# Holding four groups of mixer products later in TensorE's order, and moving elementwise work between VectorE, ScalarE and GpSimd

## The chip, the cores and the metric

The kernel runs on one core of one Trainium2 chip. A run's time is the device time of that core, in microseconds (us). TensorE (PE in the rows) does the matrix products and the transposes, VectorE is DVE, ScalarE is ACT, GpSimd is POOL, and SyncE (SP) issues nearly all DMAs.

## What is computed

Two layers over a sequence of 512 tokens of width 2048. Each layer normalises x, projects it with one large matrix, feeds four mixers of width 512, and merges them with a second large matrix:

```
h = rmsnorm(x, pre_g); proj = h @ w_in
o_a = gla_mixer(...)       # gated linear attention, chunks of 64
o_b = rglru_mixer(...)     # LRU: conv of 4 taps, gates, linear scan
o_c = nsa_mixer(...)       # sparse attention: compressed, selected, window
o_d = conformer_mixer(...) # conv of 31 taps, layernorm, silu, @ pw_w
mixed = group_rmsnorm(concat(o_a, o_b, o_c, o_d), branch_g) * silu(z gates)
x = x + rmsnorm(mixed @ w_out, post_g)
```

The LRU in full, since the change touches it (softplus(-lambda) is a vector per channel):

```
r  = sigmoid(xh @ w_a + b_a);  ig = sigmoid(xh @ w_x + b_x)
log_a = -8 * r * softplus(-lam);  a = exp(log_a)
u = sqrt(-expm1(2 * log_a)) * (ig * xc);  h = scan(h * a + u)
```

## The kernel before

Everything is kept transposed: 128 channels on the partitions, the 512 tokens along the row. A float32 product is done as three products of rounded parts (`mm3`: high*high, high*low, low*high), so each weight tile is split after it is loaded: ScalarE writes the high part `whi` (L145), VectorE or GpSimd subtracts it from the raw weights to give the low part `wlo` (L146). Which of the two engines does so is set by `pool_share`: a counter runs from 0 to 5, and a split goes to GpSimd when its number is in the tuple. `PS_A` is all six numbers, `PS_B` is (0, 3), a third.

TensorE's stream per layer: the first four columns (`f`), then 36 columns of the projection, each a sum over 16 blocks k of 128 channels, three products per block, so 48 products of 512 tokens (`pfm`, made in `proj`). In order they are 0 to 3 CONF_V, 4 to 7 LRU_X, then the products `tm` (284 wide, 16 loads of which each split is 128x284), 8 to 11 the keys and values of the sparse attention, 12 and 13 its first queries, 14 to 17 GLA's q and k, then `gv`, 18 and 19 the other queries, 20 to 35 the four gate (z) groups CONF, LRU, NSA, GLA. Then `out_ps`, the 16 columns of w_out. Between these big products stand the small ones of the mixers, which are written as Python generators (`tasks`) and advanced by a budget after each column. The chain of mixers is CONF convolutions, LRU, conformer tail, compress, group norms, attention (two rounds), its group norm, GLA, its group norm.

The order on each engine is set before the run by a planner that plays a timeline with modelled durations: big products and their accumulations have the priority "last", weight loads and splits and the evictions of columns "first", mixer work lies between. On an engine the order is then fixed, and an instruction whose inputs are late holds up all behind it. PSUM is used as eight banks: four accumulators (`acc`), three that all mixer products take in turn (`mx`), one more (`op`).

Places that the change and the prediction name: in the LRU the two gate products go to `lru_ps`, ScalarE writes sigmoid to `r` and `ig` in SBUF (L327), GpSimd multiplies `xc` by `ig` (L334) and squares `r` into `ig` (L337), VectorE makes `th` (L132, named `lth<-li,lth`), ScalarE takes its root (L340), GpSimd multiplies `xc` by it (L343), VectorE scans (L344). In the conformer tail squares are summed and split (`shi`, `slo`), the product with ones gives `var_ps`, its inverse root `lnr` (L209, L210) scales the channels (L397), Silu (L398), split, and the products `pw_ps`. In GLA `klt_ps` are four transposes, ScalarE copies them to `gklt` (L629), and `ds_ps` are seven steps of products that a chain of VectorE operations takes up (`gsp`). At the end of a layer the gated mixer outputs are split into `H` and `L` (L237, L238), which overwrite the projection's inputs, and `out_ps` reads them block by block.

Of the kernel before, what the change touches and what calls it, by code (L numbers as in the profile page):

```python
# [13 lines left out]
AF = mybir.ActivationFunctionType  # L14
# [7 lines left out]
P = 128  # L22
KT = D // P
# [35 lines left out]
PS_A, PS_B = (0, 1, 2, 3, 4, 5), (0, 3)  # L59


class Trunk:
    def __init__(self, ctx, tc, a):
        self.tc, self.nc, self.a = tc, tc.nc, a
        nc = self.nc
        self.act = nc.scalar.activation
        self.dve, self.gp = nc.vector, nc.gpsimd
        self.tr = nc.tensor.transpose
        self.bands = {"first": -2000000, "last": 2000000}
        self.tasks = []  # L70
        self.flip = 0
        self.pp = False
        self.pool_share = (0, 3)

        def pool(name, bufs, **kw):
            return ctx.enter_context(tc.tile_pool(name=name, bufs=bufs, **kw))

        con = pool("con", 1)
        self.lay = pool("lay", 1)
        self.hp = pool("hp", 1)  # L80
        self.wp = pool("wp", 3)
        self.sm = pool("sm", 4)
        self.big = pool("big", 1)
        self.acc = pool("acc", 4, space=PSUM)
        self.mx = pool("mx", 3, space=PSUM)
        self.op = pool("op", 1, space=PSUM)

        consts = con.tile([P, NCON], F32, name="consts")
        self.ident = consts[:, C_ID:C_ID + 128]
        self.tri = consts[:, C_TRI:C_TRI + 256]  # L90
        self.cmpm = consts[:, C_CMP:C_CMP + 124].rearrange("p (b n) -> p b n", b=4)
        self.glam = consts[:, C_GLA:C_GLA + 128].bitcast(U32)
        self.fold = consts[:62, C_FOLD:C_FOLD + 31]
        self.avg_d = con.tile([P, 2], F32, name="avg_d")
        self.dve.memset(self.avg_d, 1.0 / D)
        self.ones = con.tile([P, P], F32R, name="ones")
        self.dve.memset(self.ones.bitcast(F32), 1.0)
        self.consts = consts
        self.eps = con.tile([P, 1], F32, name="eps")
        self.dve.memset(self.eps, EPS)  # L100
        self.one = con.tile([P, 1], F32, name="one")
        self.dve.memset(self.one, 1.0)
        self.zero = con.tile([P, 1], F32, name="zero")
        self.dve.memset(self.zero, 0.0)
        self.warm = con.tile([P, 1], F32, name="warm")
        self.act(self.warm, self.one, AF.Exp)
        self.x1 = nc.dram_tensor("x1_scratch", (4, P, 4, S), F32, kind="Internal").ap()
# [90 lines left out]
        return self.split(self.strip("pt", "shi", 512, F32R), self.strip("pt", "slo", 512, F32R), src, self.dve)  # L198

    def mm(self, out, lhsT, rhs, start=True, stop=True, **kw):  # L200
        self.nc.tensor.matmul(out, lhsT, rhs, start=start, stop=stop, **kw)  # L201

    def mm3(self, out, ahi, alo, bhi, blo, start, stop, **kw):
        self.mm(out, ahi, bhi, start, False, **kw)
        self.mm(out, ahi, blo, False, False, **kw)
        self.mm(out, alo, bhi, False, stop, **kw)

    def rsqrt(self, out, ms, scale):
        self.act(out, ms, AF.Sqrt, bias=self.eps, scale=scale)  # L209
# [43 lines left out]
    def proj(self, c, ps=None):  # L253
        ps = self.bank("pfm", self.acc, "acc") if ps is None else ps
        u = FM_UNIT[c]
        for h in range(2):
            parts = self.unit(self.a["w_in"][self.l, u + h])
            with self.band("last"):
                for k in range(8):
                    kk = 8 * h + k  # L260
                    hi, lo = parts[k // 4]
                    w = slice(k % 4 * P, (k % 4 + 1) * P)
                    self.mm3(ps, hi[:, w], lo[:, w], self.H[kk], self.L[kk], kk == 0, kk == KT - 1)
        return ps

    def scaled(self, out, ps):
# [44 lines left out]
    def lru(self, xin):  # L311
        dve, act, gp = self.dve, self.act, self.gp
        cpos = self.lru_consts()
        xc, r, ig, th = self.quad("t2", "lxc"), self.quad("t3", "lr"), self.quad("t1", "li"), self.quad("t5", "lth")
        self.Y[LRU] = ig
        h = [slice(c * 512, (c + 1) * 512) for c in range(4)]
        yield 1.0
        for c in range(4):
            yield from self.taps(xc[:, h[c]], xin[c], 4, V_LCW + 4 * c, V_LCB + c, self.bank("lc_ps", self.op, "op"))
        whi, wlo = self.mixer_unit(self.a["lru_w"][self.l])  # L320
        for c in range(4):
            xhi, xlo = self.strip_split(xc[:, h[c]])
            for i, (o, b) in enumerate(((r, V_BA), (ig, V_BX))):
                ps = self.bank("lru_ps")
                w = slice(i * 512 + c * P, i * 512 + (c + 1) * P)
                self.mm3(ps, whi[:, w], wlo[:, w], xhi, xlo, True, True)
                act(o[:, h[c]], ps, AF.Sigmoid, bias=self.col(b + c))  # L327
            yield 1.5
        for c in range(4):
            act(th[:, h[c]], r[:, h[c]], AF.Tanh, scale=cpos[:, c:c + 1])  # L330
        self.ts(dve, cpos, cpos, -1.0, None, ALU.mult)
        for c in range(4):
            act(r[:, h[c]], r[:, h[c]], AF.Exp, scale=cpos[:, c:c + 1])
            gp.tensor_mul(xc[:, h[c]], xc[:, h[c]], ig[:, h[c]])  # L334
        yield 3.0
        for c in range(4):
            gp.tensor_mul(ig[:, h[c]], r[:, h[c]], r[:, h[c]])  # L337
        for c in range(4):
            self.stt(th[:, h[c]], ig[:, h[c]], 1.0, th[:, h[c]], ALU.add, ALU.mult)
        act(th, th, AF.Sqrt)  # L340
        yield 4.0
        for c in range(4):
            gp.tensor_mul(xc[:, h[c]], xc[:, h[c]], th[:, h[c]])  # L343
            dve.tensor_tensor_scan(ig[:, h[c]], r[:, h[c]], xc[:, h[c]], 0.0, op0=ALU.mult, op1=ALU.add)  # L344
            yield 1.5
# [23 lines left out]
    def conformer_tail(self):  # L369
        dve, gp, act, Y = self.dve, self.gp, self.act, self.Y[CONF]  # L370
        cv = [Y[:, c * 512:(c + 1) * 512] for c in range(4)]
        t_, u_ = self.strip("pt", "lnt"), self.strip("pt", "lnu")
        gp.tensor_add(t_, cv[0], cv[1])
        dve.tensor_add(u_, cv[2], cv[3])
        dve.tensor_add(t_, t_, u_)
        ps = self.chan_sum(t_, "mu_ps")
        yield 3.0
        for c in range(4):
            self.stt(cv[c], ps, -1.0 / 512, cv[c], ALU.mult, ALU.add)
            yield 0.6  # L380
        t_ = self.strip("pt", "lnt")
        act(t_, cv[0], AF.Square)
        for c in range(1, 4):
            u_ = self.strip("pt", "lnu")
            act(u_, cv[c], AF.Square)
            (gp if c == 2 else dve).tensor_add(t_, t_, u_)
        ps = self.chan_sum(t_, "var_ps")
        yield 4.0
        u_ = self.strip("yv", "lnr")
        self.rsqrt(u_, ps, 1.0 / 512)  # L390
        yield 2.0
        pb = [self.bank("pw_ps") for _ in range(3)] + [self.bank("pw_ps3", self.op, "op")]
        for h in range(2):
            phi, plo = self.mixer_unit(self.a["pw_w"][self.l, h])
            for j in range(2):
                c, s = 2 * h + j, self.strip("pt", "sy")
                (gp if j == 0 else dve).tensor_mul(s, cv[c], u_)  # L397
                act(s, s, AF.Silu, scale=self.col(V_LNG + c), bias=self.col(V_LNB + c))  # L398
                shi, slo = self.strip_split(s)
                for m in range(4):  # L400
                    w = slice(j * 512 + m * P, j * 512 + (m + 1) * P)
                    self.mm3(pb[m], phi[:, w], plo[:, w], shi, slo, h + j == 0, h + j == 2)
            yield 5.0
        for m in range(4):
            act(cv[m], pb[m], AF.Identity, bias=self.col(V_PWB + m))
        yield 3.0
# [164 lines left out]
    def gla(self, qk, gv, fg):  # L571
        dve, act, gp = self.dve, self.act, self.gp
# [20 lines left out]
        for p in range(2):  # L593
# [29 lines left out]
            act(m_, m_, AF.Exp, scale=1.0 / 16)  # L623
            gp.tensor_mul(k, k, m_)
            ps = self.bank("klt_ps")
            for b in range(4):
                self.tr(ps[:, b * P:(b + 1) * P], k[:, b * P:(b + 1) * P], self.ident)
            klT = self.strip("pt", "gklt")
            act(klT, ps, AF.Copy)  # L629
            yield 3.0  # L630
# [15 lines left out]
            for c in range(7):  # L646
                ps = self.bank("ds_ps")
                r = slice(64 * (c % 2), 64 * (c % 2) + 64)
                b = c // 2
                self.mm(ps[:, :256], klT[r, b * P:(b + 1) * P], gv[r, 512 * b + 256 * p:512 * b + 256 * p + 256])  # L650
                for h in range(2):
                    r = slice(64 * h, 64 * h + 64)
                    d = ps[r, h * P:(h + 1) * P]
# [67 lines left out]
    def layer(self, l, xs):  # L721
        nc, a, dve, act, gp = self.nc, self.a, self.dve, self.act, self.gp
        STEP = BUDGET
        STEP_N, STEP_Z = BUDGET_N, BUDGET_Z
        self.l = l
        self.Y, self.z, self.done = [None] * 4, {}, set()
        if l > 0:
            self.vec = self.nextvec
# [72 lines left out]
        self.tasks.append(self.conformer_tail())  # L801


        ptm = [self.bank(f"tm{i}", self.acc, "acc") for i in range(4)]
        for kk in range(KT):
            if kk % 2 == 0:
# [269 lines left out]
```

## Time and profile before

| | |
|---|---|
| median of 3 runs | 1648.84 us (1645.04 to 1649.55) |
| profiled execution, its own time | 1646.83 us |
| its span in the trace | 1645.0 us |
| busy PE, DVE, ACT, POOL | 1598.3, 1028.4, 726.7, 511.7 us |
| mean granted share of TensorE's clock | 0.992 |

The span runs from the first to the last instruction of the trace; the run's own time has 1.8 us around it. In the rows, a number in square brackets behind an instruction is the idle time of its engine before it and what ended it. `pfm` products overlap in the engine, so that their distance tells the rate and not their length. PEclk is the granted share of TensorE's full clock: 1.00 is 2.4 GHz, and 0.5, the lower of its two levels, 1.2 GHz.

### The profile page before, as it was taken

The numbers are of one execution on the slowest core, as the hardware profiler recorded it, in microseconds if no ns is written. First come the engines' busy times: TensorE is split into PE (matmuls) and PEld (weight loads), VectorE is DVE, ScalarE is ACT, GpSimd is POOL, SyncE is SP. The second block draws the span as 40 slices with busy tenths as digits, with TensorE's granted clock in tenths as the row PEclk, the third lists the DMA queues.
The fourth block names the chain that finished last, engine by engine and source line by source line (L and its number), as shares of the span: only waits on it lengthen the run. The fifth ranks groups of instructions, "written<-read, shape, count | busy, mean of one in ns | idle before, by whom it ended". The sixth has DMA issues, their size and how long they took to land.

```text
span 1645.0 us, 22301 instructions
## 1 busy us (share of the span) xinstructions
PE 1598.3 (97%) x8380; PEld 1354.6 (82%) x8380; DVE 1028.4 (63%) x1630; ACT 726.7 (44%) x1307; POOL 511.7 (31%) x431
## 2 busy tenths in 40 slices
PE   7999989999999999999989999999999999999996
PEld 6889867998888678888888898779988887788886
DVE  8588985487666648211396889844876576661114
ACT  6322455454455445333454224554544555453331
POOL 1454271211123323222244543611111233232223
PEclk9999999999999899999999999999999999999998
DMA  7322323422112213442243223234221222134333
GB/s 248 103 100 77 112 77 103 142 81 77 65 65 69 75 52 122 159 141 90 91 153 110 96 84 101 77 116 141 78 75 54 78 67 78 51 129 151 118 102 116
DMA packets 54859, 165.52 MB, mean 101 GB/s; under 512 B 5920, under 2 KB 14816, under 8 KB 54752
## 3 DMA queue, kind: packets, MB, share of 16 engines
q1 hardware_dynamic: 53376, 162.79, 29.8%
q8 instruction: 66, 1.08, 0.3%
q10 hardware_dynamic: 1376, 1.31, 0.2%
q14 instruction: 41, 0.34, 0.1%
HBM read 155.69 MB, written 8.39 MB: 100 GB/s over the span
## 4 chain that ended last, share of the span: by engine, by line
PE 86%; DVE 8%; ACT 2%; issue 2%; POOL 1%; DMA 1%; DVEq 0%; POOLq 0%; ACTq 0%; SPq 0%
PE pfm L201 41%; PE out_ps L201 21%; PE gv L201 6%; PE f L201 3%; PE tm L201 3%; PE o_ps L201 2%; PE s_ps L201 2%; PE pw_ps L201 1%; PE ds_ps L201 1%; PE go_ps L201 1%; DVE L L132 1%; DVE wlo L146 1%; PE pt_ps L532 1%; PE ch_ps L201 1%; PE gn_ps L201 1%
## 5 line engine op out<-in xcount | busy, mean ns | idle before, releaser
L145 ACT ACTIVATE whi<-raw 128x512 fp32r<-128x512 f32 (+1 forms) x506 | 309.5, 616 | 618.4 <-PE pfm L201 322.7
L146 POOL TENSOR_TENSOR wlo<-raw,whi 128x512 fp32r<-128x512 f32 (+1 forms) x227 | 288.0, 1271 | 800.9 <-ACT whi L145 732.9
L201 PE MATMUL pfm<-H,whi 128*128 128x512 f32 x1152 | 453.5, 394 | 0.0
L201 PE MATMUL pfm<-L,whi 128*128 128x512 f32 x1152 | 453.2, 393 | 0.0
L201 PE MATMUL pfm<-H,wlo 128*128 128x512 f32 x1152 | 452.5, 393 | 0.6 <-DVE wlo L146 0.6
L146 DVE TENSOR_TENSOR wlo<-raw,whi 128x512 fp32r<-128x512 f32 x279 | 216.9, 781 | 302.8 <-ACT whi L145 298.9
L201 PEld LDWEIGHTS pfm<-L,whi 128*128 128x128 f32 x1152 | 217.4, 189 | 46.6 <-issue 2.0
L201 PEld LDWEIGHTS pfm<-H,wlo 128*128 128x128 f32 x1152 | 217.1, 188 | 46.3 <-DVE wlo L146 1.0
L201 PEld LDWEIGHTS pfm<-H,whi 128*128 128x128 f32 x1152 | 217.2, 189 | 45.0 <-issue 0.3
L201 PE MATMUL out_ps<-H,whi 128*128 128x512 f32 (+1 forms) x552 | 201.2, 364 | 0.0
L201 PE MATMUL out_ps<-H,wlo 128*128 128x512 f32 (+1 forms) x552 | 201.2, 364 | 0.0
L201 PE MATMUL out_ps<-L,whi 128*128 128x512 f32 (+1 forms) x552 | 201.0, 364 | 0.0
L132 DVE SCALAR_TENSOR_TENSOR cv_ps<-yv,vec,cv_ps 128x512 f32<-128x512 f32 x232 | 175.2, 755 | 7.2
L201 PEld LDWEIGHTS out_ps<-H,whi 128*128 128x128 f32 x552 | 103.9, 188 | 16.7
L201 PEld LDWEIGHTS out_ps<-H,wlo 128*128 128x128 f32 x552 | 104.0, 188 | 16.6
L201 PEld LDWEIGHTS out_ps<-L,whi 128*128 128x128 f32 x552 | 103.9, 188 | 16.4
L210 DVE RECIPROCAL gn_ps<-gn_ps 128x512 f32<-128x512 f32 x32 | 107.0, 3353 | 10.1 <-ACT gn_ps L209 10.1
L201 PE MATMUL gv<-whi,L 128*128 128x256 f32 x256 | 72.6, 284 | 0.0
L201 PE MATMUL gv<-wlo,H 128*128 128x256 f32 x256 | 72.6, 284 | 0.0
L201 PE MATMUL gv<-whi,H 128*128 128x256 f32 x256 | 72.4, 283 | 0.0
L201 PE MATMUL f<-H,whi 128*128 128x256 f32 (+1 forms) x192 | 56.1, 326 | 7.3 <-ACT whi L145 7.3
L201 PE MATMUL f<-L,whi 128*128 128x256 f32 (+1 forms) x192 | 59.4, 326 | 2.2 <-DVE L L132 2.2
(292 smaller groups left out, 2354.6 us busy)
## 6 DMA issues: line engine op xcount, KB each, us to landing
raw<-w_in SPq DMA_DIRECT2D x175, 512.0 KB, 3.2
raw<-w_out SPq DMA_DIRECT2D x64, 512.0 KB, 3.6
mraw<-cmp_w SPq DMA_DIRECT2D x16, 512.0 KB, 3.7
raw<-w_tm SPq DMA_DIRECT2D x16, 284.0 KB, 2.7
xs<-xT SPq DMA_DIRECT2D x16, 256.0 KB, 5.9
xs<-xT SPq DMA_DIRECT2D x8, 512.0 KB, 4.6
x_scratch<-xs SPq DMA_DIRECT2D x16, 256.0 KB, 2.2
xs<-x_scratch SPq DMA_DIRECT2D x8, 512.0 KB, 4.7
```

What stands on the lines that cost most here:

```text
L132: self.dve.scalar_tensor_tensor(out, in0, s, in1, op0=op0, op1=op1)
L145: self.act(hi, src, AF.Copy)
L146: eng.tensor_sub(lo, src, hi.bitcast(F32))
L201: self.nc.tensor.matmul(out, lhsT, rhs, start=start, stop=stop, **kw)
L210: self.dve.reciprocal(out, out)
L532: self.tr(pt[:, (2 * j + h) * P:(2 * j + h + 1) * P], pb[h][br][:, (j0 + j) * P:(j0 + j + 1) * P], ident)
```

## The change

Four groups of small products get a tie in TensorE's order: `var_ps` not before block 13 of column 13 (`LAG`, pairs of column and block), the first quarter of `pw_ps` (channel group 0) not before block 1 of column 15, `klt_ps` of GLA's first half not before block 15 of column 31, the first `ds_ps` not before block 4 of column 32. The tie is an order without a semaphore. The LRU's input gate is written by ScalarE back into its PSUM bank, and VectorE multiplies `xc` by it there and then; the four squares go from GpSimd to ScalarE. For the `tm` stage `pool_share` is (0, 2, 4), half, in place of all.

```diff
+LAG = {"var_ps": (13, 13), "pw_ps": (15, 1), "klt_ps0": (31, 15), "ds_ps": (32, 4)}
...
     def mm(self, out, lhsT, rhs, start=True, stop=True, **kw):
-        self.nc.tensor.matmul(out, lhsT, rhs, start=start, stop=stop, **kw)
+        ins = self.nc.tensor.matmul(out, lhsT, rhs, start=start, stop=stop, **kw)
+        if self.lag:
+            self.held.setdefault(self.lag, []).append(ins.ins)
+        return ins
...
+    @contextmanager
+    def late(self, name):
+        self.lag = name if name in LAG else None
+        yield
+        self.lag = None
+
+    def release(self, ins, col, k):
+        for name, at in LAG.items():
+            if at == (col, k):
+                for i in self.held.pop(name, ()):
+                    self.tc.add_manual_dep(i, ins.name, mybir.DependencyInfo(
+                        mybir.DependencyClass.NoSync, mybir.DependencyReason.DATA), reason="late")
...
-                    self.mm3(ps, hi[:, w], lo[:, w], self.H[kk], self.L[kk], kk == 0, kk == KT - 1)
+                    ins = self.mm3(ps, hi[:, w], lo[:, w], self.H[kk], self.L[kk], kk == 0, kk == KT - 1)
+                    self.release(ins.ins, self.ncol, kk)
+        self.ncol += 1
...
-            for i, (o, b) in enumerate(((r, V_BA), (ig, V_BX))):
+            for i, b in enumerate((V_BA, V_BX)):
...
-                act(o[:, h[c]], ps, AF.Sigmoid, bias=self.col(b + c))
+                act(ps if i else r[:, h[c]], ps, AF.Sigmoid, bias=self.col(b + c))
+                if i:
+                    dve.tensor_mul(xc[:, h[c]], xc[:, h[c]], ps)
...
-            gp.tensor_mul(xc[:, h[c]], xc[:, h[c]], ig[:, h[c]])
         yield 3.0
         for c in range(4):
-            gp.tensor_mul(ig[:, h[c]], r[:, h[c]], r[:, h[c]])
+            act(ig[:, h[c]], r[:, h[c]], AF.Square)
...
-        ps = self.chan_sum(t_, "var_ps")
+        with self.late("var_ps"):
+            ps = self.chan_sum(t_, "var_ps")
...
+                with self.late(None if c else "pw_ps"):   # around the pw_ps products
...
+            with self.late(f"klt_ps{p}"):                 # around the klt_ps transposes
...
+                with self.late(None if p + c else "ds_ps"):  # around the ds_ps products
...
+        self.pool_share = (0, 2, 4)
         ptm = [self.bank(f"tm{i}", self.acc, "acc") for i in range(4)]
```

## Rows read from the trace of the kernel before

**Rows 1.** The page's first part: busy time, share, instructions of each engine.

```profile
PE 1598.3 (97%) x8380; PEld 1354.6 (82%) x8380; DVE 1028.4 (63%) x1630; ACT 726.7 (44%) x1307; POOL 511.7 (31%) x431
```

**Rows 2.** Who waited for whom, TensorE: us in total, times, longest us.

```profile
PE var_ps L201 <- DVE slo L146: 5.1, 2, 3.7
PE pw_ps L201 <- ACT shi L145: 4.4, 2, 3.8
PE ds_ps L201 <- ACT gklt L629: 3.9, 2, 2.8
...
PE ds_ps L201 <- DVE gat L640: 1.2, 1, 1.2
PE var_ps L201 <- ACT shi L145: 1.2, 2, 0.8
```

**Rows 3.** Stretches: length, busy PE PEld DVE ACT POOL, PEclk, DMA.

```profile
240.00:260.00 20.00, 18.89 (x75) 14.51 (x74) 16.38 (x15) 6.82 (x10) 6.27 (x5) 0.93 0.26 87
560.00:580.00 20.00, 17.18 (x53) 10.43 (x51) 11.27 (x22) 4.70 (x9) 5.60 (x6) 0.74 0.11 38
1060.00:1080.00 20.00, 16.16 (x66) 12.88 (x65) 13.59 (x16) 7.71 (x11) 6.44 (x5) 0.91 0.23 79
```

**Rows 4.** Timeline of TensorE: var_ps of layer 0, pw_ps of layer 1.

```profile
239.11 0.61 PE L201 MATMUL var_ps<-slo,ones 128*128 128x512 f32 x1 [3.73 <-DVE slo L146]
...
1072.77 0.80 PE L201 MATMUL pw_ps<-shi,mhi 128*128 128x512 f32 x1 [3.84 <-ACT shi L145]
```

**Rows 5.** Timeline of VectorE before var_ps, both layers.

```profile
222.10 0.68 DVE L268 TENSOR_TENSOR kv<-pfm,rbc 128x512 f32<-128x512 f32 x1
...
226.69 3.47 DVE L132 SCALAR_TENSOR_TENSOR lth<-li,lth 128x512 f32<-128x512 f32 x2
...
237.32 1.74 DVE L146 TENSOR_TENSOR slo<-lnt,shi 128x512 fp32r<-128x512 f32 x1
...
1053.91 1.76 DVE L146 TENSOR_TENSOR slo<-lnt,shi 128x512 fp32r<-128x512 f32 x1
```

**Rows 6.** Timeline of GpSimd, same place, layer 0.

```profile
217.41 1.77 POOL L334 TENSOR_TENSOR lxc<-lxc,li 128x512 f32<-128x512 f32 x1 [4.67 <-ACT li L327]
219.51 5.00 POOL L337 TENSOR_TENSOR li<-lr 128x512 f32<-128x512 f32 x4 [0.33 <-ACT lr L333]
```

**Rows 7.** Timeline of ScalarE, same place, layer 0.

```profile
221.64 0.62 ACT L382 ACTIVATE lnt<-yconf 128x512 f32<-128x512 f32 x1
...
230.20 1.92 ACT L340 ACTIVATE lth<-lth 128x2048 f32<-128x2048 f32 x1 [3.51 <-DVE lth L132]
```

**Rows 8.** Stretches, pfm products alone: length, busy PE (count).

```profile
47.00:233.70 186.70, 147.07 (x637) 119.53 (x637) 8.29 (x12) 1.00 0.29 95
...
47.00:563.50 516.50, 359.80 (x1507) 281.44 (x1507) 21.10 (x31) 1.00 0.27 89
47.00:622.70 575.70, 397.90 (x1648) 308.61 (x1649) 22.49 (x33) 0.99 0.26 86
...
866.00:1053.10 187.10, 147.02 (x637) 119.47 (x637) 8.27 (x12) 1.00 0.30 96
```

**Rows 9.** The chain that ended last, an undisturbed run: start, length, what.

```profile
56.69 87.04 PE pfm L201 x384
```

**Rows 10.** Groups by form: names, shape, count, busy us, mean ns, idle before.

```profile
L146 POOL TENSOR_TENSOR wlo<-raw,whi 128x284 fp32r<-128x284 f32 x32 | 25.2, 800 | 36.2 <-ACT whi L145 36.1
```

**Rows 11.** Stretch of the tm stage (as Rows 3); one VectorE wait there.

```profile
140.00:164.00 24.00, 24.00 (x171) 23.38 (x170) 19.39 (x27) 6.18 (x14) 10.21 (x13) 1.00 0.31 86
...
163.98 0.69 DVE L146 TENSOR_TENSOR wlo<-raw,whi 128x512 fp32r<-128x512 f32 x1 [2.90 <-ACT whi L145]
```

**Rows 12.** End of layer 0: VectorE's timeline, and out_ps by operands.

```profile
631.69 2.02 DVE L238 TENSOR_TENSOR L<-yconf,H 128x512 fp32r<-128x512 f32 x3
...
642.46 0.68 DVE L238 TENSOR_TENSOR L<-ynsa,H 128x512 fp32r<-128x512 f32 x1
...
L201 PE MATMUL out_ps<-H,whi x15: 389/389/389, 641.0 to 658.7; 128*128 128x512 f32 x15
```

More of the change, by code (lines that the diff above doesn't have):

```diff
@@ L67, in __init__ @@
         self.dve, self.gp = nc.vector, nc.gpsimd
-        self.tr = nc.tensor.transpose
         self.bands = {"first": -2000000, "last": 2000000}
@@ L200, in mm, with tr @@
     def mm(self, out, lhsT, rhs, start=True, stop=True, **kw):
-        self.nc.tensor.matmul(out, lhsT, rhs, start=start, stop=stop, **kw)
+        ins = self.nc.tensor.matmul(out, lhsT, rhs, start=start, stop=stop, **kw)
+        if self.lag:
+            self.held.setdefault(self.lag, []).append(ins.ins)
+        return ins
+    def tr(self, out, src, ident):
+        ins = self.nc.tensor.transpose(out, src, ident)
+        if self.lag:
+            self.held.setdefault(self.lag, []).append(ins.ins)
+    @contextmanager
[9 more added lines that the diff above has]
+                        mybir.DependencyClass.NoSync, mybir.DependencyReason.DATA), reason="late")
     def mm3(self, out, ahi, alo, bhi, blo, start, stop, **kw):
@@ L205, in mm3 @@
         self.mm(out, ahi, blo, False, False, **kw)
-        self.mm(out, alo, bhi, False, stop, **kw)
+        return self.mm(out, alo, bhi, False, stop, **kw)
     def rsqrt(self, out, ms, scale):
@@ L399, in conformer_tail @@
                 shi, slo = self.strip_split(s)
-                for m in range(4):
-                    w = slice(j * 512 + m * P, j * 512 + (m + 1) * P)
-                    self.mm3(pb[m], phi[:, w], plo[:, w], shi, slo, h + j == 0, h + j == 2)
+                with self.late(None if c else "pw_ps"):
+                    for m in range(4):
+                        w = slice(j * 512 + m * P, j * 512 + (m + 1) * P)
+                        self.mm3(pb[m], phi[:, w], plo[:, w], shi, slo, h + j == 0, h + j == 2)
             yield 5.0
@@ L625, in gla @@
             ps = self.bank("klt_ps")
-            for b in range(4):
-                self.tr(ps[:, b * P:(b + 1) * P], k[:, b * P:(b + 1) * P], self.ident)
+            with self.late(f"klt_ps{p}"):
+                for b in range(4):
+                    self.tr(ps[:, b * P:(b + 1) * P], k[:, b * P:(b + 1) * P], self.ident)
             klT = self.strip("pt", "gklt")
@@ L649, in gla @@
                 b = c // 2
-                self.mm(ps[:, :256], klT[r, b * P:(b + 1) * P], gv[r, 512 * b + 256 * p:512 * b + 256 * p + 256])
+                with self.late(None if p + c else "ds_ps"):
+                    self.mm(ps[:, :256], klT[r, b * P:(b + 1) * P], gv[r, 512 * b + 256 * p:512 * b + 256 * p + 256])
                 for h in range(2):
@@ L725, in layer @@
         self.l = l
+        self.ncol, self.lag, self.held = 0, None, {}
         self.Y, self.z, self.done = [None] * 4, {}, set()
```

## The prediction

> **What bounds the kernel now.** I read the page's busy times first. TensorE is busy 1598.3 of 1645.0 us, the next engine, VectorE, 1028.4 [rows 1]. So only two things can move the time: moments in which TensorE waits, and stretches in which its clock is low. The table of waits gives the first, and the reader is to see how few places there are: var_ps behind VectorE's split 5.1 us and behind ScalarE's 1.2, pw_ps 4.4, ds_ps 3.9 and 1.2 [rows 2], together 15.8 us, all over both layers, and all at small products of the mixers that stand in TensorE's order ahead of big products that were ready. The table by stretches gives the second: three of them have a granted clock under 1, and each holds or follows one of these waits [rows 3]. At half rate a stretch loses the missing share of its length: (1 - 0.93) x 20 = 1.4 us, (1 - 0.74) x 20 = 5.2 us and (1 - 0.91) x 20 = 1.8 us, together 8.4 us. What the change can win at these places is then 15.8 + 8.4 = 24.2 us of the profiled execution's 1646.83.
>
> **The change: the four ties.** What they cost is read from the distance of the tie to the place where the product stood, and from when its input was there. The pace is 87.04 us for 384 products, 0.227 us each [rows 9].
>
> var_ps stood behind 637 pfm products in either layer [rows 8]; block 13 of column 13 ends at 13 x 48 + 42 = 666, so it moves back by 29 x 0.227 = 6.6 us of TensorE's own time. Without its wait TensorE reaches the tie at about 232.9 + 6.6 = 239.5 us in layer 0, 232.9 being the end of the stretch of 637 (233.7) [rows 8] less the 0.8 of the first wait [rows 2]. The split that it needs ended at 237.32 + 1.74 = 239.06, in layer 1 at 1053.91 + 1.76 = 1055.67 [rows 5], where the tie is at 1053.1 + 6.6 = 1059.7. With VectorE's chain where it is now, the waits go, with 0.4 us in hand in layer 0 and 4.0 in layer 1.
>
> pw_ps is tied to product 15 x 48 + 6 = 726, 60 x 0.227 = 13.6 us behind the var_ps tie, at 1059.7 + 0.5 + 13.6 = 1073.8 us in layer 1, counting 0.5 for var_ps itself. Before, its input let it start at 1072.77, after 3.84 us of waiting [rows 4]. About 1 us in hand, and a var_ps that comes 4 us later could eat it, if the inverse root did not stand behind other work on VectorE. I leave 1 us of this wait per layer.
>
> ds_ps stood behind 1507 products [rows 8] and goes to 32 x 48 + 15 = 1551, 44 x 0.227 = 10.0 us later. Its input was 2.8 us late [rows 2]. Both its waits (3.9 and 1.2) and the 5.2 us of low clock behind the longer one go. klt_ps moves with it, to 1536; 15 products, 3.4 us, are left for ScalarE's copy, one operation of 0.62 us like that in rows 7 and whatever stands before it.
>
> A tie adds no semaphore. What is queued behind the held products on TensorE is the big product stream, which gains; what waits for them is the rest of the mixer chain, below.
>
> **The LRU.** GpSimd loses eight multiplies per layer (L334, L337), of 1.25 us when it runs four in a row (5.00 for four) to 1.77 [rows 6]: 8 x 1.25 = 10 us at least. VectorE gains four with one operand in PSUM: the nearest row is the column eviction of the same form, 0.68 us beside a running GpSimd [rows 5, 6], so 2.7 us; bounds 2.7 and, by the pair of 3.47 for operands both in SBUF [rows 5], 6.9. ScalarE gains four squares at 0.62 [rows 7], 2.5 us, and writes its sigmoid to PSUM in place of SBUF; no row separates the two destinations, so I bound the difference by nothing and by 0.62, one whole operation, for each of the four, 2.5 us either way, and take nothing: ScalarE idled longer than that here, 3.51 us [rows 7]. What lies on the path is the stretch from the squares to the split for var_ps: ScalarE idled 3.51 us for `lth` [rows 7], and `lth` cost 3.47 for two beside GpSimd, against about 0.7 for an operation alone [rows 5]. With the squares off GpSimd I expect `lth`, its root, the multiplies and the scans 3 to 6 us earlier.
>
> **The tm splits.** Eight per layer move from GpSimd, 0.80 us each [rows 10], to VectorE: at 0.69 for 512 wide [rows 11] about 0.4 each, 3.1 us, up to 0.8 each, 6.4 us, if they are held up as long as a GpSimd operation lasts. VectorE has 19.39 of 24 us busy there [rows 11], with convolution taps that the chain to var_ps waits for. And each split waits in VectorE's order for ScalarE's high part: one such wait was 2.90 us [rows 11]. I take 3.1 + 2 of waits, so about 5 us later for VectorE's chain; with the 2.7 above 8, against the 3 to 6 won and gaps of VectorE further on. The split for var_ps comes between 3 us earlier and 4 us later than now; I take 1 later, a wait of about half a us in layer 0 and none in layer 1.
>
> The Trainium skill ("SBUF — State Buffer", section "Who interferes with whom") speaks against this edit: a VectorE operation with two SBUF inputs and a GpSimd operation that reads SBUF shut each other out for a whole instruction. The rows of `lth` beside GpSimd agree in size (1.7 each in place of 0.7). By that rule the eight splits cost the upper end, 6.4 us, and a var_ps split 3 us later than I take; the new multiplies, with one SBUF input, would stay at 0.68, as the eviction row shows.
>
> **What is late next: the end of a layer.** Work on GLA begins 10 us later in TensorE's order, and GLA is the mixer that the layer ends with. Its last group norm product stood behind 1648 of 1728 products [rows 8], 18 us before out_ps; it would stand 8 us before. After it VectorE has some 8 us of group norm (to 630.5), and then the low parts for out_ps, from 631.69 to 642.46 + 0.68 = 643.1 [rows 12]. The last of these twelve is read at 641.0 + 11 x 3 x 0.227 = 648.5 [rows 9, 12]. So there are 5.4 us in hand against 10: at worst 4.6 us of wait per layer, at best none, because the low parts also need the projection's blocks to be done with and can change places with the group norm. I take 1.5 per layer.
>
> **The sum.** 24.2 won, less 2 (pw_ps), 0.5 (var_ps) and 3 (end of layer): 18.7 us. 1646.83 - 18.7 = 1628.1; the median of the runs lies 2.0 above the profiled execution, so 1630 us.
>
> **Rivals.** First, VectorE is late at the ties: the moved splits cost 6.4 and wait, the multiplies 6.9, and the var_ps split comes 8 us later. Then layer 0 waits 239.1 + 8 - 239.5 = 7.6 us at the tie with 5.2 of low clock, layer 1 4.0 us with 1.8. That is 18.6 in place of the 13.9 of now (5.1 + 1.2 + 4.4 + 1.4 + 1.8), and only the 10.3 us at ds_ps (3.9 + 1.2 + 5.2) is won: 5.6 less 3 at the end, 1648.84 - 2.6, about 1646. If it is 4 us late instead, layer 0 waits 3.6 and layer 1 nothing, with 1.8 of low clock: 24.2 less 5.4, 2 and 3 won, about 1635. For it: VectorE's full windows; against it: GpSimd's 10 us less. Chance 0.17, over 1635 to 1647.
>
> Second, the planner lays a new order on all engines from the change on, and its modelled durations miss somewhere else as they miss at var_ps now: five waits and three low-clock stretches cost 24.2 now, so one of the larger kind, 4 us and 5.2 of clock, in each layer would give 18.4 back. 1648.84 - 0.3, between 1648 and 1649. Against it: outside these places the table of waits is nearly empty, with the same planner. Chance 0.13. That the ties do nothing belongs here too: a tie binds only products that were emitted before its block. The conformer tail is flushed before column 12 and GLA starts by column 28, so all four bind.
>
> Third, slower: the end of the layer. If the mixer chain carries the 6.6 us of var_ps through attention to GLA and the 10.0 of ds_ps come on top, out_ps waits 16.6 - 5.4 = 11.2 us per layer, with 5.2 of low clock: 32.8 against 18.7 + 3 won, 1648.84 + 11, about 1660. It decides from 10.9 us per layer on. Against it: the ties at GLA already take up what the chain is late by, so that the larger counts and not the sum. Chance 0.10.
>
> **Chances and range.** My forecast, 1623 to 1636, has 0.60. About 0.3% (5 us) is what a measurement of this kernel can tell from no change. Faster by more than that: 0.60, 0.13 of the first rival, 0.03 of the second: 0.76. Within it: 0.04 and 0.08: 0.12. Slower: 0.02 of the second and 0.10 of the third: 0.12. The range goes down to all 24.2 us won and a few more, 1621, and up to 1648, which holds the first rival and half of the second.
>
> **What would show it.** In the profile after, the waits of TensorE should have no var_ps, pw_ps or ds_ps over 1 us, and the stretches of column 13 and 14 and of columns 31 and 32 a clock of 1.00. lth on VectorE near 0.7 each shows the LRU part right. A wait of out_ps, or low parts L238 that end after out_ps began to need them, shows the end of the layer as I fear it. A var_ps split that ends after the 666th product shows the first rival; new waits at ch_ps, gn_ps or weight splits the second. The prediction is wrong if the low clock comes back at other places, or if these waits go and the span does not shrink by them.

## The result and the profile after

The changed kernel takes 1631.97 us (median of four runs, 1629.83 to 1633.31) against 1647.07 us for the kernel before beside it (1645.04 to 1649.55): a ratio of 0.990, interval 0.9885 to 0.9915. The forecast was 1630 us, in a range of 1621 to 1648. The profiled executions are 1629.83 and 1646.83 us, their spans 1628.0 and 1645.0: 17.0 us less, where the sum said 18.7. The medians lie 15.1 us apart; the profiled execution after is the fastest of its four.

The page's first part, after, answers to [rows 1]:

```profile
PE 1591.1 (98%) x8380; PEld 1351.7 (83%) x8380; DVE 1024.5 (63%) x1654; ACT 727.1 (45%) x1313; POOL 471.9 (29%) x399
```

GpSimd lost 39.8 us. VectorE has 24 operations more and 3.9 us less: operations beside a quieter GpSimd got shorter. TensorE still bounds the kernel. Its table of waits after (what waited for what: us in total, times, longest) answers to [rows 2]:

```profile
PE pw_ps L203 <- ACT shi L147: 2.3, 2, 1.6
...
PE ds_ps L203 <- DVE gat L670: 2.1, 1, 2.1
...
PE pw_ps L203 <- DVE slo L148: 1.5, 3, 0.9
PE out_ps L203 <- DVE L L262: 0.7, 1, 0.7
PE ds_ps L203 <- ACT gklt L659: 0.5, 1, 0.5
PE pfm L203 <- POOL wlo L148: 0.3, 1, 0.3
```

No var_ps is left, and the ds_ps of layer 0 waits no more. pw_ps and the ds_ps of layer 1 still do. The stretches of [rows 3], and that of layer 1's ds_ps:

```profile
240.00:260.00 20.00, 18.03 (x72) 14.20 (x71) 15.81 (x16) 7.20 (x11) 6.28 (x5) 0.93 0.30 105
...
560.00:580.00 20.00, 20.00 (x96) 13.67 (x96) 12.71 (x25) 9.43 (x14) 12.14 (x11) 1.00 0.21 73
...
1060.00:1080.00 20.00, 18.19 (x77) 14.01 (x76) 12.68 (x17) 11.49 (x20) 3.85 (x3) 1.00 0.33 105
...
1360.00:1380.00 20.00, 17.40 (x80) 13.00 (x79) 16.27 (x22) 13.53 (x19) 13.81 (x14) 0.91 0.18 64
```

The first column after the length is TensorE's busy time, the one before the DMA share its granted clock. The two later stretches of [rows 3] run at 1.00 now. The first keeps 0.93, and 1360 to 1380 is new at 0.91. Low clock cost 8.4 us before; it costs (1 - 0.93) x 20 + (1 - 0.91) x 20 = 3.2 now. TensorE's timeline at the places with the longest waits, pw_ps of layer 0 and ds_ps of layer 1:

```profile
254.95 0.50 PE L203 MATMUL pw_ps<-shi,mhi 128*128 128x512 f32 x1 [1.61 <-ACT shi L147]
...
1371.83 0.69 PE L203 MATMUL ds_ps<-gv,gklt 64*128 64x256 f32 x2 [0.50 <-ACT gklt L659]
...
1375.29 0.70 PE L203 MATMUL ds_ps<-gv,gklt 64*128 64x256 f32 x2 [2.10 <-DVE gat L670]
```

VectorE's timeline before var_ps of layer 0 answers to [rows 5]:

```profile
219.81 0.68 DVE L355 TENSOR_TENSOR lxc<-lxc,lru_ps 128x512 f32<-128x512 f32 x1
...
223.75 3.00 DVE L134 SCALAR_TENSOR_TENSOR lth<-li,lth 128x512 f32<-128x512 f32 x3
...
227.27 0.68 DVE L134 SCALAR_TENSOR_TENSOR lth<-li,lth 128x512 f32<-128x512 f32 x1
...
234.29 1.78 DVE L148 TENSOR_TENSOR slo<-lnt,shi 128x512 fp32r<-128x512 f32 x1
235.99 6.64 DVE L371 TENSOR_TENSOR_SCAN li<-lr,lxc 128x512 f32<-128x512 f32 x3
242.56 0.66 DVE L148 TENSOR_TENSOR wlo<-raw,whi 128x512 fp32r<-128x512 f32 x1
243.14 1.21 DVE L371 TENSOR_TENSOR_SCAN li<-lr,lxc 128x512 f32<-128x512 f32 x1
```

The gate's multiply (first line) takes 0.68 us. Three `lth` take 3.00 us together and the fourth 0.68, where two took 3.47 [rows 5] and the other two 0.68 and 0.92. The split `slo` that var_ps needs ends at 236.07; it ended at 239.06 [rows 5]. It is 3.0 us earlier and TensorE gets to var_ps at 239.08, so 3.0 us are in hand. Behind it stand the LRU's scans, and behind three of these a split of a big weight, `wlo`.

That order is new. The first scan before (first line), against the change's ScalarE root, which the scans wait for by way of GpSimd's multiplies, and TensorE's first product with the low part of the 55th weight tile of the projection (a tile serves 12 products; this one matters below):

```profile
233.50 2.29 DVE L344 TENSOR_TENSOR_SCAN li<-lr,lxc 128x512 f32<-128x512 f32 x1 [2.14 <-POOL lxc L343]
...
230.53 1.92 ACT L367 ACTIVATE lth<-lth 128x2048 f32<-128x2048 f32 x1
...
235.44 0.39 PE L203 MATMUL pfm<-H,wlo 128*128 128x512 f32 x1
```

Before, `slo` stood behind the first scan; now it stands ahead of all four. The root starts at 230.53, before at 230.20 [rows 7], and the first scan at 235.99, before at 233.50: neither is earlier. The product at 235.44 runs before the first scan starts, so its weight split stood ahead of the scans too.

By stages: the first out_ps of layer 0 moves from 641.0 [rows 12] to 626.8, that of layer 1 from 1454.0 to 1436.8:

```profile
L203 PE MATMUL out_ps<-H,whi x552: 277/389/392, 626.8 to 1612.5; 128*128 128x512 f32 x142, 128*128 128x256 f32 x42
```

So layer 0 is 14.2 us ahead where its end begins, about 1 us is given back there, and layer 1 adds 4.2. Counted product by product, layer 0's gain is 4.3 us in the conformer stage and 9.5 in the GLA stage; layer 1 gains some 4 us in all, none of them at GLA.

### The profile page after: what moved, and what is told of

Read it like the earlier page. It is cut to its first block, busy times and chain, and to the rows that moved or that the text cites. A ratio compares the mean times of both kernels' runs of the same rounds, so it can differ in the third digit from the quotient of the medians.

```text
span 1628.0 us, 22310 instructions
## 1 busy us (share of the span) xinstructions
PE 1591.1 (98%) x8380; PEld 1351.7 (83%) x8380; DVE 1024.5 (63%) x1654; ACT 727.1 (45%) x1313; POOL 471.9 (29%) x399
## 4 chain that ended last, share of the span: by engine, by line
PE 88%; DVE 7%; ACT 2%; DMA 2%; issue 1%; POOL 0%; SPq 0%; DVEq 0%; POOLq 0%; ACTq 0%
PE pfm L203 44%; PE out_ps L203 20%; PE gv L203 6%; PE tm L203 3%; PE f L203 2%; PE o_ps L203 2%; PE s_ps L203 2%; PE pw_ps L203 1%; DVE L L134 1%; PE go_ps L203 1%; PE pt_ps L209 1%; DVE wlo L148 1%; PE ch_ps L203 1%; PE ds_ps L203 1%; PE gn_ps L203 1%
## 5 line engine op out<-in xcount | busy, mean ns | idle before, releaser
L148 POOL TENSOR_TENSOR wlo<-raw,whi 128x512 fp32r<-128x512 f32 (+1 forms) x211 | 276.5, 1311 | 805.1 <-ACT whi L147 761.9
L148 DVE TENSOR_TENSOR wlo<-raw,whi 128x512 fp32r<-128x512 f32 (+1 forms) x295 | 225.8, 769 | 318.9 <-ACT whi L147 308.5
L203 PEld LDWEIGHTS out_ps<-L,whi 128*128 128x128 f32 x552 | 104.0, 188 | 17.7 <-DVE L L262 1.1
```

What stands on the lines that cost most here:

```text
L148: eng.tensor_sub(lo, src, hi.bitcast(F32))
L203: ins = self.nc.tensor.matmul(out, lhsT, rhs, start=start, stop=stop, **kw)
```

## The experiments

**My theory** was the prediction's: the ties take the small products from the head of TensorE's queue, the LRU's move lets their inputs come in time, and the moved splits cost VectorE a little. **The rivals**: the ties do it all; the moves do it all; what ends a layer takes the gain back. The first four kernels ran on one chip beside the kernel before (1650.07 us), the next four beside 1649.28, the last four beside 1647.34. The kernel before differs by 3 us from group to group, so that across groups the ratios to it count, not the medians alone.

**Ties alone.** The LRU and the tm splits as before.

```diff
...
-                act(ps if i else r[:, h[c]], ps, AF.Sigmoid, bias=self.col(b + c))
-                if i:
-                    dve.tensor_mul(xc[:, h[c]], xc[:, h[c]], ps)
+                act(o[:, h[c]], ps, AF.Sigmoid, bias=self.col(b + c))
...
+            gp.tensor_mul(xc[:, h[c]], xc[:, h[c]], ig[:, h[c]])
...
-            act(ig[:, h[c]], r[:, h[c]], AF.Square)
+            gp.tensor_mul(ig[:, h[c]], r[:, h[c]], r[:, h[c]])
...
-        self.pool_share = (0, 2, 4)
```

> Only the four ties; the LRU gate, the squares and the weight splits of the tm stage stay where they were. Theory A (the ties win, the moved work only makes inputs earlier): the split for var_ps ends as before, at 239.1 us in layer 0, the tie stands at 239.5, so the waits at var_ps go and most of pw_ps and ds_ps too: 1630 to 1637 us. Theory B (the relief of GpSimd brings the time, the ties little): 1643 to 1648 us.

Measured 1638.55 us, 0.993 (0.9911 to 0.9949): between the two. The var_ps wait is gone, but its place is taken. TensorE's waits, VectorE's timeline and the stretch:

```profile
PE pfm L203 <- DVE wlo L148: 8.4, 2, 7.7
```

```profile
237.30 1.74 DVE L148 TENSOR_TENSOR slo<-lnt,shi 128x512 fp32r<-128x512 f32 x1
238.97 4.41 DVE L370 TENSOR_TENSOR_SCAN li<-lr,lxc 128x512 f32<-128x512 f32 x2
243.31 0.66 DVE L148 TENSOR_TENSOR wlo<-raw,whi 128x512 fp32r<-128x512 f32 x1
```

```profile
240.00:260.00 20.00, 15.98 (x62) 13.01 (x63) 13.05 (x14) 6.64 (x10) 5.14 (x4) 0.83 0.31 106
```

`slo` ends where it did before, in time for the tie. But TensorE, no longer held at var_ps, now reaches the big product whose weight split `wlo` stands on VectorE behind two scans, and waits 7.7 us there, with (1 - 0.83) x 20 = 3.4 us of low clock behind it. Before, the var_ps wait of 3.73 [rows 4] gave that split its time. The same product, the first that needs the low part of the 55th weight tile, before and with ties alone:

```profile
244.06 0.49 PE L201 MATMUL pfm<-H,wlo 128*128 128x512 f32 x1 [0.57 <-DVE wlo L146]
...
244.02 0.80 PE L203 MATMUL pfm<-H,wlo 128*128 128x512 f32 x1 [7.72 <-DVE wlo L148]
```

It starts at the same time in both, so in layer 0 the tie at var_ps alone wins nothing up to here. In layer 1 it does what it was meant to: var_ps no longer waits, the longest wait left at a weight split is 0.7 us, and the stretch from 1060 to 1080 us is back at full clock (before 0.91 [rows 3]).

**Moves alone.** The change without ties.

```diff
-LAG = {"var_ps": (13, 13), "pw_ps": (15, 1), "klt_ps0": (31, 15), "ds_ps": (32, 4)}
+LAG = {}
```

> The moved work without any tie. Theory A: the waits at ds_ps with the low clock behind them (10.3 us before) stay, var_ps and pw_ps wait 3 to 5 us less than the 10.7 of before: 1640 to 1646 us. Theory B: 1630 to 1635 us.

Measured 1640.53 us, 0.9943 (0.9925 to 0.9961), as expected for moves that don't do it alone. Without a tie the wait goes on to the next small products:

```profile
PE pw_ps L203 <- ACT shi L147: 6.0, 2, 4.1
...
PE klt_ps L209 <- POOL qk L653: 3.0, 2, 2.7
PE ds_ps L203 <- ACT gklt L659: 2.3, 1, 2.3
```

**The tm splits back on GpSimd**, the rest of the change kept.

```diff
-        self.pool_share = (0, 2, 4)
```

> The change, but all weight splits of the tm stage stay on GpSimd. If the eight splits cost VectorE's chain the 5 us of the prediction, the split for var_ps comes up to 5 us earlier, but the ties already cover it, so the time is the change's within 2 us: 1630 to 1634. If half the splits on VectorE are needed, because GpSimd was late with them, 1636 or more.

Measured 1628.92 us, 0.9868 (0.9849 to 0.9887): a little under what was expected. VectorE's timeline:

```profile
231.90 1.78 DVE L148 TENSOR_TENSOR slo<-lnt,shi 128x512 fp32r<-128x512 f32 x1
```

The split ends 2.4 us earlier than in the change, and the stretch from 240 to 260 us has no low clock. The ratio is 0.003 under the change's (0.990), with intervals that just touch: this part of the change seems to cost some 3 us. The kernel without it is the base of most kernels below.

**The LRU back on GpSimd**, ties and moved splits kept (the first two parts of the first diff).

> The change, but the LRU gate and its squares are back on GpSimd; ties and splits as changed. Theory A: the split for var_ps, 236.1 us in layer 0 of the change, ends 5 to 8 us later, past the tie at 239, so that var_ps waits 2 to 5 us again in layer 0 and pw_ps with it: 1635 to 1642 us. If the ties alone carry the gain, 1630 to 1634.

Measured 1636.17 us, 0.9916 (0.9899 to 0.9933): the time that was expected, but not for the reason. `slo` ends at 237.48, 1.4 us later than in the change, and var_ps does not wait. TensorE's waits, and VectorE's scans in layer 0:

```profile
PE pfm L203 <- POOL wlo L148: 2.8, 1, 2.8
PE pw_ps L203 <- ACT shi L147: 2.4, 1, 2.4
```

```profile
237.40 7.76 DVE L370 TENSOR_TENSOR_SCAN li<-lr,lxc 128x512 f32<-128x512 f32 x4
```

Beside ties alone, measured on the same chip, it is 2.4 us faster, with no overlap of the runs (up to 1637.13 against 1637.68 and more): with the LRU on GpSimd the moved splits win, where with the LRU moved they seem to cost. And the 7.7 us wait of ties alone is gone without the LRU's move: the product that waited there runs at 235.88, ahead of all four scans. What took it away here is the place of its split in the planner's order.

**All sixteen tm splits on VectorE**, for a dose.

```diff
-        self.pool_share = (0, 2, 4)
+        self.pool_share = ()
```

> The change with all sixteen tm splits of a layer on VectorE in place of half. If the moved splits cost the change its 3 us against all on GpSimd (1632.0 to 1628.9) by pushing VectorE's convolutions back, eight more push them back as far again: the split for var_ps ends after its tie in layer 0 and the time is 1634 to 1642 us. If the 3 us come from the planner's other order, the time need not follow the number of splits: 1628 to 1634.

Measured 1635.73 us, 0.993 (0.9916 to 0.9944). With 0, 8 and 16 splits per layer on VectorE: 1628.9, 1632.0, 1635.7 us; 0.9868, 0.990, 0.993. The convolution of layer 0 ends at 186.8, 188.6 and 192.3 us. The time is in the expected range by another wait than expected: `slo` ends at 238.33, in time for the tie, and the longest pw_ps wait is 3.6 us here. Each split is short. VectorE's splits of this width from 140 to 166 us (count, busy us, mean ns, idle before), of the change and of this kernel:

```profile
L148 DVE TENSOR_TENSOR wlo<-raw,whi 128x284 fp32r<-128x284 f32 x6 | 3.0, 492 | 1.4 <-ACT whi L147 1.4
```

```profile
L148 DVE TENSOR_TENSOR wlo<-raw,whi 128x284 fp32r<-128x284 f32 x13 | 5.7, 451 | 1.5 <-ACT whi L147 1.3
```

**The squares back on GpSimd, and the gate back** (its sigmoid to SBUF, its multiply on GpSimd), each on the kernel with the tm splits undone; the diff is of the squares.

```diff
-            act(ig[:, h[c]], r[:, h[c]], AF.Square)
+            gp.tensor_mul(ig[:, h[c]], r[:, h[c]], r[:, h[c]])
```

> All four ties, tm splits on GpSimd, the gate in PSUM and its multiply on VectorE, but the four squares back on GpSimd. If the squares are what made lth late (3.5 us of idle ScalarE, lth at 1.7 each beside GpSimd), scans and weight splits are late again and TensorE waits for a split in column 13 or 14, as the 7.7 us seen with ties alone: 1633 to 1639 us. If the gate is what counts: 1627 to 1631.

> All four ties, tm splits on GpSimd, the squares on ScalarE, but the gate in SBUF and its multiply on GpSimd again. If the squares are what counts: 1627 to 1632 us. If the gate's multiplies on GpSimd, which stand ahead of the squares' users there, hold the stage up by themselves: 1633 to 1639.

Measured 1637.45 us, 0.9937 (0.9922 to 0.9951), and 1638.73 us, 0.9944 (0.9929 to 0.9959): either half undone loses what both undone do (ties alone, 0.993); with both in place it is 0.9868. Half of the loss or a little more is seen on TensorE and VectorE around 240 us, here of the kernel with the gate back:

```profile
240.39 0.80 PE L203 MATMUL pfm<-H,wlo 128*128 128x512 f32 x1 [4.04 <-DVE wlo L148]
```

```profile
232.59 2.30 DVE L370 TENSOR_TENSOR_SCAN li<-lr,lxc 128x512 f32<-128x512 f32 x1
...
236.45 2.28 DVE L370 TENSOR_TENSOR_SCAN li<-lr,lxc 128x512 f32<-128x512 f32 x1
238.65 1.68 DVE L148 TENSOR_TENSOR wlo<-raw,whi 128x512 fp32r<-128x512 f32 x1
```

The squares' kernel waits 3.42 us for the same split, at 241.15. In both, `slo` was in time. It is the weight split behind two scans that is late, as with ties alone. With the low clock after it this costs 5 to 6 us of TensorE's time in the conformer stage of layer 0, against 1.0 with both halves in place. The rest is at ds_ps of layer 0, 2.9 us of waiting in either and a low clock that the base does not have there:

```profile
560.00:580.00 20.00, 17.13 (x73) 12.11 (x72) 15.14 (x22) 11.60 (x15) 14.62 (x14) 0.83 0.23 79
```

Layer 1's ds_ps loses less than in the base in return. Why the planner's order changes so with half of the LRU is not shown.

**Conformer ties alone**, in the change and with the tm splits undone.

```diff
-LAG = {"var_ps": (13, 13), "pw_ps": (15, 1), "klt_ps0": (31, 15), "ds_ps": (32, 4)}
+LAG = {"var_ps": (13, 13), "pw_ps": (15, 1)}
```

> The change with the ties of var_ps and pw_ps alone; klt_ps and ds_ps are free. If the two pairs of ties act each in its own stage, this lies between no ties (1640.5 us) and the change (1632): the conformer pair saves the 4.1 us wait at pw_ps of layer 1 with its low clock and part of layer 0's, some 5 us, so 1634 to 1637 us. If the mixer chain, moved back by the conformer ties, reaches GLA's old place later, klt_ps and ds_ps wait longer than the 3.0 and 2.3 us seen without ties, and it is 1640 or more.

> All tm splits on GpSimd and only the conformer ties. The GLA ties were worth nothing with half the splits moved (1632.3 without, 1632.0 with). If that holds here, this is 1628.9 within 2 us: 1627 to 1631. If ds_ps tied alone (1626.2) is what gains, it is 1629 or more, by 3 us over that kernel.

Measured 1632.34 us, 0.9903 (0.9887 to 0.9919), and 1629.24 us, 0.990 (0.9878 to 0.9921). The first is under both of its ranges and equal to the change: there the two ties at GLA are worth nothing that can be measured. The second is equal to its base by the median (1628.92) and 0.003 above it by the ratio, with intervals that overlap, so that it doesn't settle the point. Nor do these two show a price of the tm splits by their ratios (0.9903 and 0.990). The pfm products ahead of klt_ps before, without any tie, and in the first of the two kernels:

```profile
47.00:555.80 508.80, 357.20 (x1497) 279.64 (x1497) 20.44 (x30) 1.00 0.27 89
...
47.00:556.10 509.10, 357.93 (x1507) 280.40 (x1507) 20.50 (x30) 1.00 0.27 89
...
47.00:557.58 510.58, 362.95 (x1527) 283.84 (x1527) 21.21 (x31) 1.00 0.27 90
```

Before, klt_ps stood behind 1497 of them. Without a tie of its own it now comes behind 1527, next to where the tie would put it (1536). Ten of the 30 products come without any tie; the other 20 are the work of the two conformer ties, which carry the mixers' chain back, GLA with it. Which of the two does so is not shown.

**klt_ps untied**, ds_ps kept, tm splits undone.

```diff
-LAG = {"var_ps": (13, 13), "pw_ps": (15, 1), "klt_ps0": (31, 15), "ds_ps": (32, 4)}
+LAG = {"var_ps": (13, 13), "pw_ps": (15, 1), "ds_ps": (32, 4)}
```

> All tm splits on GpSimd, klt_ps free, ds_ps tied as in the change. If klt_ps late is what makes gklt late for ds_ps in layer 1 (1.5 us) and at_ps and gat with it (2.1 us), both waits go, and klt_ps waits up to 3 us for GpSimd in each layer again: 1625 to 1631 us. If gat is late by itself, the ds_ps wait stays and klt_ps waits too: 1631 to 1635.

Measured 1626.21 us (1626.0 to 1627.32), 0.9865 (0.9848 to 0.9882): the lowest time of all, and 5.8 us under the change, but in its ratio the same as with klt_ps tied (0.9868). As expected, ds_ps waits no more and klt_ps waits for GpSimd again (2.3 us in layer 1); the wait for `gat` has moved on to go_ps (2.4). The stretch at var_ps and pw_ps is clean in it, that of layer 1's ds_ps as in the change:

```profile
240.00:260.00 20.00, 19.03 (x80) 14.59 (x79) 15.80 (x17) 7.82 (x12) 5.96 (x4) 1.00 0.31 104
...
1360.00:1380.00 20.00, 17.59 (x83) 13.89 (x83) 13.41 (x20) 11.12 (x14) 13.12 (x13) 0.91 0.15 53
```

**ds_ps later**, by 5 blocks (3.4 us) and by 16 (10.9 us), tm splits undone, to test the end of the layer.

```diff
-"ds_ps": (32, 4)}
+"ds_ps": (32, 9)}
...
-"ds_ps": (32, 4)}
+"ds_ps": (33, 4)}
```

> All tm splits on GpSimd, and the first ds_ps tied to block 9 of column 32 in place of block 4, 15 products or 3.4 us later. Theory A: the 2.1 us wait for gat and the 1.5 for gklt in layer 1, with the low clock behind them (10.2 us at half rate in the profile of the kernel with the tie at 4, 5.1 lost), go: 1628.9 less 4 to 8, 1621 to 1625 us. Theory C (the end of the layer has no room, as the third rival has it): out_ps waits 2 to 4 us per layer more and gives it back: 1627 to 1632.

> All tm splits on GpSimd, and the first ds_ps tied to block 4 of column 33: 48 products or 10.9 us later than in the change. This measures the room at the end of the layer. By the prediction's working 5.4 us were in hand against the 10.0 of the change's own tie, so 10.9 more would show as 8 to 11 us of waits at out_ps in each layer, with low clock: 1640 to 1655 us. If the room is larger than that (only 0.7 us of wait was seen at out_ps), 1622 to 1630.

Measured 1633.59 us, 0.9912 (0.9897 to 0.9928), and 1632.06 us, 0.990 (0.9882 to 0.9917): both outside the ranges of either theory. TensorE's waits in the first, then in the second:

```profile
PE go_ps L203 <- DVE gat L670: 4.1, 1, 4.1
...
PE out_ps L203 <- DVE L L262: 2.9, 2, 2.6
```

```profile
PE go_ps L203 <- DVE gat L670: 4.2, 1, 4.2
PE out_ps L203 <- ACT H L261: 3.4, 2, 3.1
```

ds_ps no longer waits, but VectorE's `gat` is awaited a product further on, at go_ps, and out_ps waits. Both lose 3 to 5 us by medians against their base, and 6 to 7 against the kernel with klt_ps free, on the same chip. The loss does not grow from 3.4 us later to 10.9: the end of a layer does not pass a shift on one for one, as I had reckoned for the second kernel. How GLA's later products came to be early enough there is not settled.

## Why the prediction was right, point by point

The forecast (1630 us) and the range hold, and the time fell by 17.0 us of span and 15.1 of medians where the sum said 18.7. The reading behind it holds too: TensorE's waits and low clock were the only stock to win from. By the same two views, low clock fell from 8.4 to 3.2 us, and TensorE's listed waits from 17.1 to 7.4, those of f, rb_ps and rs_ps apart, which hardly changed (17.7 and 17.5). That is 14.9 of the 17.0 us won; where the other 2 lie is not assigned. That the total came out so near is in part luck: at the places that the sum names, 9.6 us of the 24.2 are left where 2.5 were expected, against 0.7 at the end of the layers where 3 were, and two steps of the working were wrong.

- **"With VectorE's chain where it is now, the waits go."** Wrong as a reason. It holds in layer 1, where 4.0 us were in hand. In layer 0 ties alone leave 7.7 us of waiting at a weight split in place of var_ps. I had looked at the product that waited, not at the splits behind it in VectorE's order. In the change that split stands ahead of the scans, which start no earlier (235.99 us, with ties alone 233.45). Of the kernels examined for it, those where it stands ahead (the change, the tm splits undone, the LRU undone) don't wait there, and those with ties where it stands behind (ties alone, either half of the LRU undone) do. The order is the planner's, and every edit lays it anew; that the LRU's relief by itself earns the gain is not shown.
- **The var_ps split "between 3 us earlier and 4 us later", 1 later taken.** It came 3.0 earlier, the favourable end; the 0.5 us for var_ps was not paid. But it did not come by the path that the prediction gave, `lth`, its root, the multiplies and the scans 3 to 6 us earlier. The last `lth` ends 2.2 us earlier (227.95, before 230.16) and ScalarE's wait for it [rows 7] is gone (the two slow `lth` of [rows 5] had begun after the squares ended, at 224.51 [rows 6], so they ran beside GpSimd's other work), yet the root starts 0.3 us later and the first scan 2.5 later. `slo` is earlier because it no longer stands behind the first scan in VectorE's order. That was not forecast: here the term came out by luck.
- **The multiplies at 0.68.** Right: 0.68 [rows 5] before for the form, 0.68 after.
- **The tm splits, "about 5 us later" with the 3.1 us of their own.** Right in direction by the dose above, about 3 us of kernel time; the pair of kernels without the GLA ties does not show it, and with the LRU on GpSimd they win 2.4. They cost 0.45 to 0.49 us each on the mean, near the lower bound of 0.4. The upper bound took GpSimd to be at work beside every split, and it hardly was: of the six splits of the change listed above, one ran beside a GpSimd operation. It took 0.70 us, the others 0.45. The Trainium skill's rule ("SBUF — State Buffer", "Who interferes with whom") speaks of operations that overlap in time, and the trace agrees; the prediction applied it to all eight.
- **pw_ps: 2 us left.** It left 2.3 + 1.5 us and 1.4 of low clock in layer 0. With the tm splits undone 1.9 and no low clock are left, so the excess seems to be theirs.
- **ds_ps: both waits and the low clock go.** They went in layer 0 and stayed in layer 1: 2.6 us of waiting, 1.8 of low clock. The low clock there is new. And the ties at GLA were not needed to bring the change's time: without them it is the same, because the chain arrives later by itself.
- **The end of a layer: 3 us.** 0.7 us of waiting, and about 1 us of layer 0's lead. The third rival's ground against itself fits what was seen: the two shifts do not add up.
- **The rivals.** VectorE late at the ties: not in the change, and with all sixteen splits moved at pw_ps (4.3 us), not at var_ps. The planner's order: in the change the new loss is small (ds_ps of layer 1, 2.6 us of waiting where there were 2.3, and 1.8 of low clock). But the planner's order is what decides in the other kernels: in ties alone it leaves the awaited split behind the scans, as it was before the change, and that cost 7.7 us and 3.4 of low clock.
- **The signs named beforehand.** Not all came. pw_ps (1.61 us) and ds_ps of layer 1 (2.10) still wait over 1 us, and a low clock came back at a new place, in layer 1's ds_ps, which was a sign of being wrong. It cost 1.8 us, too little to undo the rest.

## What to carry to other kernels

A queue that waits at its head covers everything behind it: before a wait is taken away, list what the engine will reach next, and on which engine and behind which work that item's input stands. Here a wait of 3.7 us came back as 7.7 at a weight split behind two scans, and it was gone where the planner put that split ahead of them. So after every edit, read where the split stands before crediting the work that was moved. On one chip, held products alone won 11.5 us, the moves alone 9.5, ties and the LRU without the moved splits 21.2; and the change did as well with its two early ties alone.

## What the runs showed of the hardware

VectorE's operations with both inputs in SBUF were lengthened where a GpSimd operation ran beside them. With GpSimd idle the 128x284 splits took 0.45 to 0.46 us each; the one in the change that began 0.4 us into a pair of GpSimd's took 0.70, here VectorE's line and then GpSimd's:

```profile
148.50 0.70 DVE L148 TENSOR_TENSOR wlo<-raw,whi 128x284 fp32r<-128x284 f32 x1 [0.16 <-ACT whi L147]
...
148.09 1.76 POOL L148 TENSOR_TENSOR wlo<-raw,whi 128x284 fp32r<-128x284 f32 x2 [6.21 <-ACT whi L147]
```

The 128x512 splits took 0.66 to 0.69 us free and up to 1.78 beside GpSimd. In the kernel before, one that began at 224.99 us, 0.5 us into a GpSimd operation, ended at 226.77, 0.55 us after that operation did (226.22): it looks as if it had waited for the rest of it and then run. A scan of 128x512 took 2.2 to 2.3 us while GpSimd ran and 1.21 at 243.14 in the change, with GpSimd idle: work on GpSimd nearly doubled the scans that stand ahead of a split on VectorE.

The clock's price depends on more than the longest wait. The ds_ps of layer 1 waited 0.50 and 2.10 us in the change and 1.54 and 2.08 in the kernel with the tm splits undone, 3.4 us apart in both. The stretch of the first stands above at 0.91, 1.8 us lost; that of the second:

```profile
1360.00:1380.00 20.00, 16.38 (x67) 11.62 (x65) 13.40 (x19) 11.04 (x14) 13.31 (x14) 0.75 0.15 53
```

That is 5.0 us lost, about 10 us at half the full rate, for 1 us more of waiting. So that kernel, among the best here, has this stretch still to win.
